# Seven half-size products in the output projection of a hybrid decoder step

## The chip, the core and the metric

The kernel runs on one core of a Trainium2 chip: TensorE (PE, with PEld for the weight loads that overlap it), VectorE (DVE), ScalarE (ACT), GpSimd (POOL), and SyncE (SP), which issues all DMAs of this kernel in one queue. The metric is device time in microseconds, median of several executions. Before the change it is 2507.13 us (three runs, 2505.12 to 2507.76).

## What is computed

One layer of a decoder with 16 heads of three kinds, over 1024 prompt tokens (with 16 meta tokens ahead of them) and 8 x 8 sample tokens, in float32. Every column comes from one input projection; after the heads comes the output projection, to which the change belongs, then the residual and a final norm.

```python
    h = _rmsnorm(x, norm_w)
    proj = jnp.einsum('bld,de->ble', h, w_in)
    (aq, ak, av, ao, ai, af, bq, bk, bv, ba, bb, cq, cf, ci, z) = jnp.split(proj, SPLIT_POINTS, axis=-1)
...
    hcat = jnp.concatenate([ha, hb, hc], axis=2)
    hcat = hcat * lax.rsqrt(jnp.mean(hcat * hcat, axis=-1, keepdims=True) + EPS)
    y = hcat.reshape(bsz, L, MIX) * out_norm_w.astype(f32) * jax.nn.silu(z.astype(f32))
    out = jnp.einsum('ble,ed->bld', y.astype(x.dtype), w_out)
    return x + out, (st_a[0], st_a[1], st_a[2], st_b, new_conv, st_c)
...
    y_prompt = _rmsnorm(xp[:, N_META:], final_norm_w)
    y_sample = _rmsnorm(xs, final_norm_w)
```

w_out is 2048 x 2048: 16 heads of 128 rows by four column groups of 512.

## The kernel before

**Precision.** Each float32 operand of a large product is split into a high and a low part in a format that TensorE takes at one pass, and a product is the sum of three matmuls: high·high, high·low and low·high. A weight block of 128 x 512 is loaded as a tile wraw (`o_raw` for w_out, `w_raw` for w_in), cast to whi on ACT and subtracted to wlo on DVE (`feed_split`). `pieces` lists all blocks in order of use; `feed_ahead` keeps three of them split and seven loaded or asked for ahead of the one in use, in four buffers each.

**Stages.** The prompt goes through in two halves of 512 tokens (`Half`; the first one also holds the sample and meta tokens). For each half `run_group` computes the input projection head by head, in the fixed ORDER (17 entries, "C3" the last), from the normalized transposed input hT/hB into PSUM tiles acc. While TensorE goes on with the next head, the last head's recurrence runs as a *stream*: a Python generator (`mlstm_scan`, `gdn_scan`, `hgrn_scan`, then `finish`) that gives out a few instructions at each step. `Weave` holds four queues of such streams (scan, fin, post, bg); `pump`, called between matmuls, takes a step when its due time on the estimated clock `ck` has come, and `drain` runs streams to their end. The build then fixes the order on each engine from the order of the source and from when its own model has an instruction ready, so a load can stand well ahead of its place in the source. bg holds `prep_B`, which prepares the second half's input in the first part of the run with tiles px and pxs.

**Finish.** `finish` scales one head's output by its norm, turns it around through DRAM (yd), multiplies by the gate into y, splits y into high (cast on ACT) and low (subtraction on POOL), and stores both parts to `y_dram`.

**Output projection.** `load_y` brings a half's y back, two heads to a tile, into the buffers h that held hT; the first half's comes in during the last input group, the second half's during the fourth unit. Then nine units (OUT_UNITS): for the first half four column groups with five token tiles each (one of samples), for the second half four with four tiles, of which the last is cut into two of two tiles. A unit runs over 16 heads; each weight block serves all its tiles:

```python
                    T.matmul(accs[n], yh, whi, start=k == 0, stop=False)
                    T.matmul(accs[n], yh, wlo, start=False, stop=both and k == NK - 1)
                    if not both:
                        T.matmul(accs[n], yl, whi, start=False, stop=k == NK - 1)
```

The samples' high and low parts share one stationary block, so they need two matmuls. A unit's accumulators (oacc, one PSUM bank of eight each) are added on DVE to a block of the input x (tile res), squared and summed on ACT, and multiplied by the final norm's weights on POOL. After a half's last column group `final_norm` scales the blocks and stores them.

## Time and profile before

| | us |
|---|---|
| median of 3 runs | 2507.13 |
| the profiled execution, its own time | 2506.0 |
| its span, first to last instruction | 2504.3 |
| mean granted TensorE clock | 0.990 |
| first half (input projection, heads) | 0 to about 1166 |
| second half | about 1166 to 2102.3 |
| output projection (first to last oacc matmul) | 2102.3 to 2493.9 |
| from the last matmul to the end | 10.4 |

All operations go through one helper, so all lines of the profile carry L137 and groups are told apart by the tile they write. A group's row reads: line, engine, operation, output <- inputs, shapes, count, then busy time, the mean of one in ns, and the idle time of the engine just before it with what ended it. A row of a window reads: start and end, length, then busy time and count for PE, PEld, DVE, ACT, POOL (of one tile's instructions alone where a tile is asked for), granted clock, DMA share and GB/s. Busy times of matmuls overlap each other, since they are pipelined.

### The profile page before, as it was taken

How to read it: one execution, taken by the hardware profiler on the slowest of the kernel's cores; microseconds unless marked ns; L12 is line 12 of the kernel's file. 1: busy time of each engine (PE TensorE's matmuls, PEld its weight loads, DVE VectorE, ACT ScalarE, POOL GpSimd, SP SyncE). 2: the span in 40 equal slices, each digit the busy share in tenths (PEclk: the TensorE clock that was granted, in tenths of full speed). 3: DMA queues.
4: the chain of work that ended last, by engine and by line, in shares of the span. 5: the costliest groups of instructions: out<-in, count | busy, mean ns of one | idle time of the engine just before them, and what ended most of it. 6: DMA issues, size and time to landing. Idle time of an engine off the chain costs nothing.

```text
span 2504.3 us, 43941 instructions
## 1 busy us (share of the span) xinstructions
PE 2442.1 (98%) x16032; PEld 2184.5 (87%) x16032; DVE 1425.5 (57%) x3080; ACT 991.2 (40%) x2430; POOL 554.8 (22%) x743
## 2 busy tenths in 40 slices
PE   6999999999999999999999999999999999999998
PEld 5898999999999999999787888888888888888886
DVE  7775655765656655556864556554654545323435
ACT  5643434443435333333642434333443334222324
POOL 5331212420313312113320113110320102211201
PEclk9999999999999999999999999999999999999999
DMA  5656665655645454447554455454554558636735
GB/s 129 152 140 147 147 146 133 162 131 130 158 99 138 99 131 118 118 119 203 132 132 115 120 123 136 122 130 101 138 127 114 129 123 257 183 84 200 254 97 185
DMA packets 681045, 350.82 MB, mean 140 GB/s; under 512 B 260004, under 2 KB 622076, under 8 KB 680828
## 3 DMA queue, kind: packets, MB, share of 16 engines
q1 hardware_dynamic: 680828, 348.01, 54.3%
q8 instruction: 126, 2.06, 0.4%
q14 instruction: 91, 0.75, 0.1%
HBM read 285.71 MB, written 62.19 MB: 139 GB/s over the span
## 4 chain that ended last, share of the span: by engine, by line
PE 80%; issue 5%; DVE 5%; DMA 4%; ACT 2%; POOL 2%; SPq 1%; POOLq 0%; DVEq 0%; ACTq 0%
PE acc L137 59%; PE oacc L137 9%; PE pa L137 1%; DVE wlo L137 1%; PE po L137 1%; PE nd L137 1%; PE pz L137 1%; PE pyy L137 1%; DMA wraw<-in_w_in_dram 1%; POOL res L137 1%; PE pu L137 1%; DMA px<-in_x_prompt_dram 1%; ACT whi L137 1%; PE poh L137 1%; PE pw L137 1%
## 5 line engine op out<-in xcount | busy, mean ns | idle before, releaser
L137 DVE TENSOR_TENSOR wlo<-wraw,whi 128x512 fp32r<-128x512 f32 x720 | 525.6, 734 | 569.6 <-ACT whi L137 552.1
L137 PE MATMUL acc<-hA,whi 128*128 128x288 f32 (+1 forms) x4544 | 826.2, 304 | 11.3 <-ACT whi L137 6.4
L137 ACT CAST whi<-wraw 128x512 fp32r<-128x512 f32 x720 | 441.9, 618 | 929.1 <-PE acc L137 641.2
L137 PE MATMUL acc<-hB,whi 128*128 128x512 f32 x2272 | 722.2, 400 | 4.3 <-ACT whi L137 2.1
L137 PEld LDWEIGHTS acc<-hA,whi 128*128 128x128 f32 x4544 | 679.6, 191 | 18.2 <-ACT whi L137 8.1
L137 PE MATMUL acc<-hA,wlo 128*128 128x288 f32 x2240 | 489.7, 299 | 1.6 <-DVE wlo L137 1.6
L137 PEld LDWEIGHTS acc<-hB,whi 128*128 128x128 f32 x2272 | 413.6, 189 | 86.2 <-ACT whi L137 2.7
L137 PE MATMUL acc<-hB,wlo 128*128 128x512 f32 x1120 | 441.1, 394 | 2.6 <-DVE wlo L137 2.6
L137 PEld LDWEIGHTS acc<-hA,wlo 128*128 128x128 f32 x2240 | 367.7, 190 | 2.7 <-DVE wlo L137 2.6
L137 PE MATMUL oacc<-whi,y 128*128 128x512 f32 x1088 | 343.4, 390 | 1.1 <-ACT whi L137 1.1
L137 PEld LDWEIGHTS acc<-hB,wlo 128*128 128x128 f32 x1120 | 211.0, 188 | 52.0 <-DVE wlo L137 6.8
L137 PEld LDWEIGHTS oacc<-whi,y 128*128 128x128 f32 x1088 | 204.2, 188 | 44.5 <-ACT whi L137 2.4
L137 PE MATMUL oacc<-wlo,y 128*128 128x512 f32 x576 | 224.8, 390 | 1.2 <-DVE wlo L137 1.2
L137 PEld LDWEIGHTS oacc<-wlo,y 128*128 128x128 f32 x576 | 108.1, 188 | 25.2 <-DVE wlo L137 3.1
L137 POOL TENSOR_TENSOR res<-res,fnw 128x512 f32<-128x512 f32 (+1 forms) x34 | 54.3, 1627 | 255.4 <-ACT oscr L137 255.4
L137 POOL TENSOR_TENSOR y<-y,zs 128x592 fp32r<-128x592 f32 (+1 forms) x32 | 46.0, 1437 | 171.4 <-ACT zs L137 106.7
L137 POOL TENSOR_TENSOR qd<-qT,emb 128x512 f32<-128x512 f32 x12 | 17.7, 1479 | 230.3 <-PE po L137 230.3
L137 DVE TENSOR_TENSOR Yt<-Yc,Bb 128x60 f32<-128x60 f32 (+8 forms) x180 | 37.6, 209 | 43.9 <-DMA Bb<-db 39.0
L137 POOL TENSOR_TENSOR hr<-hr,halfneg 128x4 f32<-128x4 f32 (+1 forms) x48 | 44.1, 919 | 61.1 <-DVE hr L137 58.4
L137 POOL TENSOR_TENSOR nrm<-nrm,halfneg 128x10 f32<-128x10 f32 x12 | 23.5, 1960 | 138.9 <-DVE nrm L137 138.9
L137 POOL TENSOR_TENSOR X<-Ex,hk 128x256 f32<-128x256 f32 (+1 forms) x40 | 39.1, 978 | 63.2 <-PE pa L137 41.8
L137 ACT ACTIVATE Wt<-pw,nrm 128x128 f32<-128x128 f32 (+1 forms) x54 | 19.8, 367 | 78.1 <-PE pw L137 78.1
(416 smaller groups left out, 2766.7 us busy)
## 6 DMA issues: line engine op xcount, KB each, us to landing
wraw<-in_w_in_dram SPq DMA_DIRECT2D x564, 256.0 KB
wraw<-in_w_out_dram SPq DMA_DIRECT2D x144, 256.0 KB
y<-y SPq DMA_DIRECT2D x16, 576.0 KB
px<-in_x_prompt_dram SPq DMA_DIRECT2D x32, 256.0 KB
yd<-y SPq DMA_DIRECT2D x128, 64.0 KB
out_dram<-sst SPq DMA_DIRECT2D x16, 512.0 KB
s<-yd SPq DMA_DIRECT2D x32, 256.0 KB
y<-zs SPq DMA_DIRECT2D x32, 256.0 KB
```

The lines of the kernel that those rows point to most:

```text
L137: return f(out, *a, **k)
```

## The change

The output projection of the 1024 prompt tokens is written as a product of 2 x 2 blocks: rows A1x, A2x are the two token halves, columns of A and rows of B the two sets of heads K1 (the first eight in ORDER) and K2 (the other eight), columns of B two pairs of column groups. Seven products of half size and sums give the four result blocks:

- S1 = A21 + A22, S2 = S1 - A11, S3 = A11 - A21, S4 = A12 - S2, in `finish` of the second half, from unsplit copies of y kept in `y_whole`; S1 to S4 and A22 are then split and stored in `y_comb`. The split's subtraction is now on DVE for these.
- T1 = B12 - B11, T2 = B22 - T1, T3 = B22 - B12, T4 = T2 - B21 (up to the order of subtraction in the code), on POOL, in a new bg stream `combine_weights` during the second half, stored in `w_comb`.
- The products, in order: A11·B11, A12·B21, S2·T2, S1·T1, S4·B22, S3·T3, A22·T4. Each is two units (j = 0, 1) of four tiles over eight heads; the last unit is cut in two. The sample tokens' rows are not combined: their matmuls ride along with the first three products, sharing a weight block (`own`) or with one of their own (`other`), so there they use one or two banks more.
- `load_y` brings in the next left factor while another one is in use. Partial results t1 and q stay in SBUF, and the input x is added at different places, by DVE or POOL.

```diff
-OUT_UNITS = ([(cg, range(5)) for cg in range(4)], [(cg, range(4)) for cg in range(3)] + [(3, range(2)), (3, range(2, 4))])
+HEADS = [{"A": 0, "B": HA, "C": HA + HB}[name[0]] + int(name[1]) for name in ORDER[1:]]
+K1, K2 = HEADS[:NH // 2], HEADS[NH // 2:]
+LAST_UNITS = [(0, range(4)), (1, range(2)), (1, range(2, 4))]
...
+    def c_raw(name, j, kk):
+        raw = wp.tile([P, 512], F32, tag="wraw", name="wraw")
+        DMA(raw, w_comb[name][NK // 2 * j + kk])
+        return raw
...
+    w_comb = {n: dp.tile([NK, P, 512], F32, name=n) for n in ("T1", "T2", "T3", "T4")}
+    y_comb = {n: dp.tile([NK // 2, P, 2 * HALF], F32R, name=n) for n in ("S1", "S2", "S3", "S4", "A22")}
+    y_whole = [dp.tile([n, P, HALF], F32, name=f"yw{n}") for n in (NH, NK // 2)]
...
-    for units in OUT_UNITS:
-        for cg, _ in units:
-            for k in range(NK):
-                pieces.append((o_raw, k, cg))
+    def out_pieces(j, rows, cg):
+        return [(o_raw, head, cg) for head in rows]
+    for j in range(2):
+        pieces += out_pieces(j, K1, j)
+    for j in range(2):
+        for a, b in zip(out_pieces(j, K2, j), out_pieces(j, K1, j + 2)):
+            pieces += [a, b]
+    for j in range(2):
+        for kk, b in enumerate(out_pieces(j, K2, j + 2)):
+            pieces += [(c_raw, "T2", j, kk), b]
+    for j in range(2):
+        pieces += [(c_raw, "T1", j, kk) for kk in range(NK // 2)]
+    for j in range(2):
+        pieces += out_pieces(j, K2, j + 2)
+    for j in range(2):
+        pieces += [(c_raw, "T3", j, kk) for kk in range(NK // 2)]
+    for j, _ in LAST_UNITS:
+        pieces += [(c_raw, "T4", j, kk) for kk in range(NK // 2)]
...
+        if not half.first:
+            kk, upper = HEADS.index(head) % (NK // 2), head in K1
+            ya = sp.tile([P, 512], F32, tag="vx0", name="ya", bufs=1)
+            if not upper:
+                yb = sp.tile([P, 512], F32, tag="vx1", name="yb", bufs=1)
+                yc = sp.tile([P, 2, 512], F32, tag="sst", name="yc", bufs=1)
+                yc, spare = yc[:, 0], yc[:, 1].bitcast(F32R)
...
+        if not half.first:
+            DMA(ya, y_whole[0][K1[kk]])
+            if not upper:
+                DMA(yb, y_whole[1][kk])
+                DMA(yc, y_whole[0][head])
...
+        if half.first:
+            DMA(y_whole[0][head], y[:, 0:HALF])
+            S.copy(yhi[:, 0:W], y[:, 0:W])
+            yield
+            yield
+            G.tensor_tensor(ylo[:, 0:W], y[:, 0:W], yhi[:, 0:W], op=ALU.subtract)
+            yield
+            d = y_dram[head].bitcast(F32)
+            for part, t in enumerate((yhi, ylo)):
+                t = t.bitcast(F32)
+                DMA(d[:, 2 * NSAMP + HALF * part:2 * NSAMP + HALF * (part + 1)], t[:, 0:HALF])
                 DMA(d[:, NSAMP * part:NSAMP * (part + 1)], t[:, HALF:WS])
+            return
+        y, yhi = y[:, 0:HALF], yhi[:, 0:HALF]
+        def parts(src, hi, name):
+            S.copy(hi, src)
+            ck.sync()
+            V.tensor_tensor(src.bitcast(F32R), src, hi, op=ALU.subtract)
+            d = y_comb[name][kk].bitcast(F32)
+            ck.last += 1.0
+            yield
+            DMA(d[:, 0:HALF], hi.bitcast(F32))
+            DMA(d[:, HALF:], src)
+        if upper:
+            DMA(y_whole[1][kk], y)
+            G.tensor_tensor(ya, ya, y, op=ALU.subtract)
+            yield
+            yield from parts(ya, yhi, "S3")
+            return
+        G.tensor_tensor(yb, yb, y, op=ALU.add)
+        yield
+        yield from parts(y, yhi, "A22")
+        G.tensor_tensor(ya, yb, ya, op=ALU.subtract)
+        yield
+        yield from parts(yb, spare, "S1")
+        G.tensor_tensor(yc, yc, ya, op=ALU.subtract)
+        yield
+        yield from parts(ya, yhi, "S2")
+        yield
+        yield from parts(yc, spare, "S4")
...
+    def load_y(u, n, src):
+        t = hp.tile([P, 2, 2 * NSAMP + 2 * HALF], F32R, tag=f"h{2 * u + n // 2}{n % 2}", name=f"y{u}{n}")
+        for q in range(2):
+            kk = 2 * n + q
+            if isinstance(src, str):
+                DMA(t[:, q, 2 * NSAMP:].bitcast(F32), y_comb[src][kk].bitcast(F32))
+            else:
+                DMA(t[:, q].bitcast(F32), y_dram[src[kk]].bitcast(F32))
+        yT[u][n] = t
+    def y_block(u, kk, n, part):
+        at_ = 2 * NSAMP + HALF * part + P * n
+        return yT[u][kk // 2][:, kk % 2, at_:at_ + P]
+    def combine_weights():
+        for j in range(2):
+            for kk in range(NK // 2):
+                b11, b12, b21 = (sp.tile([P, 512], F32, tag="px", name="px", bufs=3) for _ in range(3))
+                b22 = sp.tile([P, 512], F32, tag="pxs", name="pxs", bufs=1)
+                for t, heads, cg in ((b11, K1, j), (b12, K1, j + 2), (b22, K2, j + 2), (b21, K2, j)):
+                    DMA(t, i["w_out"][0, P * heads[kk]:P * (heads[kk] + 1), 512 * cg:512 * (cg + 1)])
+                for dst, a, b in ((b11, b12, b11), (b12, b22, b12), (b22, b22, b11), (b21, b21, b22)):
+                    ck.last = ck.t["T"] + 7.0
+                    yield
+                    G.tensor_tensor(dst, a, b, op=ALU.subtract)
+                ck.last = ck.t["T"] + 4.0
+                yield
+                for n, t in (("T1", b11), ("T3", b12), ("T2", b22), ("T4", b21)):
+                    DMA(w_comb[n][NK // 2 * j + kk], t)
+                ck.last = ck.t["T"] + 10.0
+                yield
...
+            weave.add("bg", combine_weights())
...
+    def phase(u, accs, tiles, own=None, other=None, each=None):
+        for kk in range(NK // 2):
+            whi, wlo = next_piece()
+            for n in tiles:
+                yh, yl = (y_block(u, kk, n, part) for part in (0, 1))
+                T.matmul(accs[n], yh, whi, start=kk == 0, stop=False)
+                T.matmul(accs[n], yh, wlo, start=False, stop=False)
+                T.matmul(accs[n], yl, whi, start=False, stop=kk == NK // 2 - 1)
+                if n == tiles[0]:
+                    feed_ahead()
+                weave.pump()
+            for job in (own, other):
+                if not job:
+                    continue
+                if job is other:
+                    whi, wlo = next_piece()
+                a, block = job
+                T.matmul(a, block(kk), whi, start=kk == 0, stop=False)
+                T.matmul(a, block(kk), wlo, start=False, stop=kk == NK // 2 - 1)
+                if job is other:
+                    feed_ahead()
+                weave.pump()
+            if each:
+                each(kk)
+    def banks(tiles=halfn):
+        return {n: bank("oacc") for n in tiles}
...
+    t1, q = {}, {}
+    for j in range(2):
+        accs, sacc = banks(), bank("oacc")
+        phase(0, accs, halfn, own=(sacc, lambda kk: yT[0][kk // 2][:, kk % 2, 0:2 * NSAMP]))
+        ck.begin()
+        if j == 0:
+            weave.drain_queue("bg")
+            for n in halfn:
+                t1[j, n] = sp.tile([P, 512], F32, tag="px" if n < 3 else "pxs", name="t1", bufs=3 if n < 3 else 1)
+                S.copy(t1[j, n], accs[n])
+            held = sacc
+    weave.drain_queue("scan")
+    weave.drain_queue("fin")
+    weave.drain_queue("post")
+    ys = [row(tag, "ys", F32R)[:, 0:512] for tag in "aabb"]
...
+    fnw += [sp.tile([P, 512], F32, tag=f"s{t}", name="fnw", bufs=1) for t in ("7", "8", "9", "B")]
+    ck.begin()
+    for n in halfn:
+        t1[1, n] = free.pop(0)
+        S.copy(t1[1, n], accs[n])
+    for t, c in zip(fnw, range(4)):
+        DMA(t, i["final_norm_w"][512 * c:512 * (c + 1)].rearrange("(x d) -> x d", x=1).partition_broadcast(P))
+    for c in range(4):
+        DMA(ys[c].bitcast(F32).rearrange("p (h c) -> p h c", h=4), y_dram[4 * c:4 * (c + 1), :, 0:2 * NSAMP].bitcast(F32).rearrange("h p c -> p h c"))
+    def ys_block(heads):
+        return lambda kk: ys[heads[kk] // 4][:, P * (heads[kk] % 4):P * (heads[kk] % 4 + 1)]
+    sample_add(0, held, False)
+    sample_add(1, sacc, False)
+    weave.add("bg", norm_states())
+    for j in range(2):
+        accs, sacc, sacc2 = banks(), bank("oacc"), bank("oacc")
+        def each(kk):
+            if j == 0 and kk in (1, 3, 5):
+                load_y(0, kk // 2, "S2")
+        phase(1, accs, halfn, own=(sacc, lambda kk: yT[1][kk // 2][:, kk % 2, 0:2 * NSAMP]), other=(sacc2, ys_block(K1)), each=each)
+        weave.drain_queue("bg")
+        for n in halfn:
+            t = res[n + 1, j] = x_load(n + 1, j)
+            ck.begin()
+            V.tensor_tensor(t, t, accs[n], op=ALU.add)
+            G.tensor_tensor(t, t, t1[j, n], op=ALU.add)
+            squared(n + 1, j)
+        sample_add(j, sacc, True)
+        sample_add(j + 2, sacc2, False)
+    for j in range(2):
+        accs, sacc = banks(), bank("oacc")
+        def each(kk):
+            if j == 0 and kk == 1:
+                load_y(0, 3, "S2")
+            if j == 0 and kk in (3, 5, 7) or j == 1 and kk == 1:
+                load_y(1, kk // 2 - 1 if j == 0 else 3, "S1")
+        phase(0, accs, halfn, other=(sacc, ys_block(K2)), each=each)
+        for n in halfn:
+            ck.begin()
+            V.tensor_tensor(t1[j, n], t1[j, n], accs[n], op=ALU.add)
+        sample_add(j + 2, sacc, True)
+    free += [row(tag, "res")[:, 0:512] for tag in "aabb"]
+    weave.add("post", final_norm([0], range(4)))
+    for j in range(2):
+        accs = banks()
+        def each(kk):
+            if j == 0 and kk % 2:
+                load_y(0, kk // 2, "S4")
+        phase(1, accs, halfn, each=each)
+        for n in halfn:
+            q[j, n] = free.pop(0)
+            ck.begin()
+            V.tensor_tensor(q[j, n], t1[j, n], accs[n], op=ALU.add)
+    weave.drain_queue("post")
+    for j in range(2):
+        accs = banks()
+        def each(kk):
+            if j == 0 and kk % 2:
+                load_y(1, kk // 2, "S3")
+        phase(0, accs, halfn, each=each)
+        for n in halfn:
+            t = res[n + 1, j + 2] = free.pop(0)
+            ck.begin()
+            V.tensor_tensor(t, q[j, n], accs[n], op=ALU.add)
+            x = x_load(n + 1, j + 2)
+            G.tensor_tensor(t, t, x, op=ALU.add)
+            free.append(x)
+            squared(n + 1, j + 2)
+            x = x_load(n + 5, j)
+            G.tensor_tensor(t1[j, n], t1[j, n], x, op=ALU.add)
+            free.append(x)
+    weave.add("post", final_norm(range(1, 5), range(4)))
+    for j in range(2):
+        accs = banks()
+        def each(kk):
+            if j == 0 and kk % 2:
+                load_y(0, kk // 2, "A22")
+        phase(1, accs, halfn, each=each)
+        for n in halfn:
+            t = res[n + 5, j + 2] = q[j, n]
+            ck.begin()
+            V.tensor_tensor(t1[j, n], t1[j, n], accs[n], op=ALU.add)
+            V.tensor_tensor(t, t, accs[n], op=ALU.add)
+            x = x_load(n + 5, j + 2)
+            G.tensor_tensor(t, t, x, op=ALU.add)
+            free.append(x)
+            squared(n + 5, j + 2)
+    weave.drain_queue("post")
+    for j, tiles in LAST_UNITS:
+        accs = banks(tiles)
+        phase(0, accs, tiles)
+        weave.drain_queue("post")
+        late = tiles[-1] == NC - 1 and j == 1
+        for n in tiles:
+            t = res[n + 5, j] = t1[j, n]
+            ck.begin()
+            V.tensor_tensor(t, t, accs[n], op=ALU.add)
+            squared(n + 5, j, late)
+        if j == 1:
+            weave.add("post", final_norm([n + 5 for n in tiles], (2, 3, 0, 1), late))
     weave.drain_queue("bg")
     weave.drain_queue("post")
```

140 lines of the change are left out of this document (52 added, 88 removed).

## Prediction

> **What bounds the kernel now.** I read the page first (busy shares, the chain that ended last), then the groups of instructions, then TensorE's waits, then windows of the stage that the change rewrites.
>
> ```profile
> span 2504.3 us, 43941 instructions
> PE 2442.1 (98%) x16032; PEld 2184.5 (87%) x16032; DVE 1425.5 (57%) x3080; ACT 991.2 (40%) x2430; POOL 554.8 (22%) x743
> PE 80%; issue 5%; DVE 5%; DMA 4%; ACT 2%; POOL 2%; SPq 1%; POOLq 0%; DVEq 0%; ACTq 0%
> L137 PE MATMUL oacc<-whi,y 128*128 128x512 f32 x1088 | 343.4, 390 | 1.1 <-ACT whi L137 1.1
> L137 PE MATMUL oacc<-wlo,y 128*128 128x512 f32 x576 | 224.8, 390 | 1.2 <-DVE wlo L137 1.2
> ```
>
> TensorE is busy 98% of the span and holds 80% of the last chain; no other engine passes 57%. The output projection is the tile oacc: 1088 + 576 = 1664 matmuls of 128x512, with 1.1 + 1.2 us of idle time in front of them. The mean of 390 ns is the length of one in the pipeline, not the pitch, so the pitch comes from windows. The waits of TensorE from 2100 us to the end, the oacc row with its first and last start, and then four windows of the tile oacc (length, busy time and count of PE, PEld, DVE and ACT, clock, DMA share, GB/s):
>
> ```profile
> PE oacc L137 <- DVE wlo L137: 1.2, 5, 0.3
> PE oacc L137 <- ACT whi L137: 1.1, 3, 0.7
> ```
> ```profile
> L137 PE MATMUL oacc<-whi,y x1088: 387/389/529, 2102.3 to 2493.5; 128*128 128x512 f32 x182
> ```
> ```profile
> 2203.10:2253.50 50.40, 50.40 (x224) 41.72 (x223) 3.22 (x5) 0.58 (x1) 1.00 0.32 84
> 2253.50:2303.90 50.40, 50.40 (x224) 41.75 (x223) 3.22 (x5) 0.58 (x1) 1.00 0.60 187
> 2310.00:2330.20 20.20, 19.82 (x87) 15.84 (x85) 3.22 (x5) 0.58 (x1) 1.00 0.59 185
> 2472.00:2493.90 21.90, 20.28 (x83) 14.89 (x81) 0.67 (x1) 0.00 (x0) 1.00 0.65 207
> ```
>
> 224 matmuls take 50.40 us: 225 ns each, with nothing between them, although each of the first two windows holds a change of unit. So in this stage a matmul less is 225 ns less, as long as the weight pieces, the evacuations and the transfers keep up. Only the end is worse: 83 matmuls in 21.90 us, where the pitch asks 18.7.
>
> **The change: what goes.** Before, 8 prompt tiles x 16 heads x 4 column groups x 3 products (hi·hi, hi·lo, lo·hi) = 1536 matmuls, plus 128 for the samples. After, 7 products x 2 column groups x 4 tiles x 8 heads x 3 = 1344, plus the same 128. That is 1472, and 192 fewer: 192 x 0.225 = **43.2 us**. The pieces go from 144 to 152; each needs a cast on ACT and a subtraction on DVE as before, and I cost them at nothing, since TensorE spends at least 1.35 us on a piece of 6 matmuls and 3.2 us on a pair of pieces of 14.
>
> **What is added beside the second token half** (1215 to 2102 us). The window over all engines, the groups that do the same operations today, the DMA issue of a weight block, and a window of the first half, which already carries a background stream through px:
>
> ```profile
> 1215.00:2102.00 887.00, 881.53 (x4936) 728.16 (x4936) 501.42 (x1047) 340.99 (x803) 158.87 (x180) 1.00 0.52 131
> L137 POOL TENSOR_TENSOR y<-y,zs 128x512 fp32r<-128x512 f32 (+1 forms) x16 | 21.4, 1338 | 123.8 <-ACT zs L137 76.9 <-DMA wraw<-in_w_in_dram 45.4 <-issue 1.5
> L137 DVE TENSOR_TENSOR wlo<-wraw,whi 128x512 fp32r<-128x512 f32 x274 | 202.4, 743 | 194.1 <-ACT whi L137 188.0 <-PE acc L137 3.6 <-DMA hvT<-hvT 1.4
> L137 ACT CAST zs<-y x32: 604/646/689, 203.3 to 2171.9; 128x592 fp32r<-128x592 f32 x16, 128x512 fp32r<-128x512 f32 x16
> wraw<-in_w_out_dram SPq DMA_DIRECT2D x144, 256.0 KB
> 400.00:676.00 276.00, 273.37 (x2194) 269.00 (x2193) 177.52 (x404) 114.91 (x309) 78.29 (x107) 0.98 0.62 146
> ```
>
> - The weight combinations: 16 rounds of 4 POOL subtractions, 64 x 1.34 = 86 us. The heads: 8 upper ones keep one POOL operation, 8 lower ones have three for one, 16 x 1.34 = 21 us. POOL goes from 159 to 266 of 887 us, 30%.
> - The splits: 8 + 8 x 4 = 40 on DVE (30 us, 501 to 531) and 24 casts more on ACT (16 us).
> - DMA: 16 x 8 blocks of 0.262 MB = 33.6 MB for the weights; the heads load and store 31.5 MB where they stored 8.4. Together 57 MB more, 131 to 195 GB/s, and some 220 issues more in SP's queue. (In the first half 16 blocks are stored more, 4.2 MB in 1100 us; I count nothing.)
>
> None of it is in TensorE's stream; what hides it is the 881.5 us of matmuls and a fetch of seven pieces ahead. If the cover fails, the longer chains of a head (up to four splits one after the other at its end, which hold the zs and y buffers longer) reach the next head's scan, and SP's queue, standing at a store that waits for POOL, holds back the weight loads behind it. The lower bound is nothing. For the upper one I take the window 400 to 676, at 28% POOL and 146 GB/s: 2.63 us idle and a clock of 0.98, thus 8.2 us lost in 276, where this half loses 5.5 in 887. Carried over, 26 us less 5.5, about 20. I take 3, near the low end, since this half has 40% of DVE's time free.
>
> **What is added in the output stage.** There are 15 units where there were nine, and sums that stay in SBUF: 56 DVE additions from PSUM for 32, and 62 POOL operations on prompt tiles for 30. Today's durations, by tile and by group from 2100 us:
>
> ```profile
> L137 DVE TENSOR_TENSOR res<-res,oacc x36: 671/679/689, 2160.4 to 2493.9; 128x512 f32<-128x512 f32 x32, 64x512 f32<-64x512 f32 x4
> L137 POOL TENSOR_TENSOR res<-res,fnw 128x512 f32<-128x512 f32 x30 | 46.4, 1568 | 255.4 <-ACT oscr L137 255.4
> ```
>
> DVE: four evacuations of 0.68 us in a unit of 21.6 us. POOL is thickest in the fifth product: 24 x 1.57 = 38 of 43 us. It lags there without holding a bank, because DVE's addition frees the bank and x is added afterwards. The narrow places are the second product, whose unit takes six of the eight banks (before, five), and the end of the first, where four copies on ACT free the banks behind the last head's finish. The next unit can start in the two free banks; two tiles are 1.35 us of matmuls, and the old unit's first tile ends 2.9 us ahead of the unit's end, so a bank comes free in time unless its addition waits for an x block. A change of unit costs 0 in the two clean windows and 0.6 us (20.20 less 87 x 0.225) where the old stage passed from one half to the other. For 14 changes that is 0 to 8 us; I take 3, the rows lying nearer to nothing.
>
> The tail: the last two units have 8 pieces instead of 16, so seven of eight are fetched before the unit starts. That can win back the 3.2 us lost today; or the outputs of the two tiles before (2.1 MB, 6.4 us at 328 GB/s) stand ahead of the last outputs and cost up to 6. I take +1. The chain from the last matmul (2493.9) to the end, 10.4 us, stays.
>
> **The sum.** The profiled execution took 2506.0 us, 1.7 more than its span and 1.1 below the median of the three (2507.13). 2506.0 - 43.2 + 3 + 3 + 1 = 2469.8, so **2470 us**.
>
> **Transfers, the price that could undo it.** Per product, in MB (pieces + y blocks + x and outputs) and us of matmuls: second 13.9 to 18 (with ys, the norm weights and the last head's blocks) in 57.7; third 13.6 in 50.4; fourth 8.9 in 43.2; fifth 12.6 in 43.2; sixth 14.7 in 43.2; seventh 8.4 in 43.2. That is 312, 270, 206, 292, 340 and 194 GB/s at most, where the old stage has 168 on average. The busiest windows today and the whole stage, all engines; then a window with a clock below 1 and TensorE's waits in it; then a piece of the chain that ended last (start, length):
>
> ```profile
> 2330.20:2363.00 32.80, 32.79 (x145) 27.15 (x146) 14.53 (x25) 10.76 (x23) 2.39 (x2) 1.00 0.94 328
> 2340.00:2350.00 10.00, 10.00 (x46) 8.29 (x45) 2.77 (x4) 2.84 (x5) 0.00 (x0) 1.00 0.98 361
> 2102.00:2504.00 402.00, 389.54 (x1768) 320.75 (x1767) 162.79 (x263) 131.91 (x260) 78.05 (x62) 0.99 0.55 168
> 580.00:680.00 100.00, 98.14 (x808) 96.07 (x809) 60.02 (x146) 37.68 (x105) 22.58 (x37) 0.95 0.58 139
> ```
> ```profile
> PE pz L137 <- DVE Yc L137: 2.2, 1, 2.2
> ```
> ```profile
> 2478.12 5.50 DMA wraw<-in_w_out_dram
> ```
>
> 328 GB/s for 32.8 us with TensorE never idle: the load exists today and costs nothing. The Trainium skill (DMA: Bandwidth & Descriptors, Specifications) puts the limit of HBM for one core at about 358 GB/s; the 361 of the 10 us window agrees with it as a ceiling. By that figure no product is bound by transfers, and the sum would stay.
>
> **The rivals.**
> 1. *Transfers bind in the output stage; slower.* If only a rate R is reached, a product lasts MB/R: at 0.25 the second, third, fifth and sixth lose 14.3 + 4.0 + 7.2 + 15.6 = 41 us, so at about 248 GB/s the gain is gone. At the 207 of the tail, in which the last chain runs through 5.50 us of a weight load, they lose 29.3 + 15.3 + 17.7 + 27.8 = 90: 2506.0 - 43.2 + 90 = 2553; halfway, at 228, about 2527. For it: y blocks of half a megabyte stand ahead of weight pieces in one queue, and idle time lowers the clock (0.95 in the window with the 2.2 us wait). Against it: the 328 above, and most y blocks have a whole unit of slack. Chance 0.12.
> 2. *The second half's side work reaches TensorE.* The upper price of 20 us in place of 3: 2487. For it, the longest chain of a head grows by some 15 us of splits; against it, 18% to 30% of POOL and free DVE. Chance 0.20.
> 3. *Nothing new waits, and the tail's 3.2 us come back:* 2506.0 - 43.2 - 3.2 = 2459.6. Chance 0.08.
>
> That the products are not fewer is excluded by the count.
>
> The Trainium skill (SBUF — State Buffer, Who interferes with whom) speaks against the change: a DVE operation with two SBUF inputs and a POOL operation that reads SBUF lock each other out. By it, the added 80 POOL operations could hold up DVE by as much as 107 us in the second half, an estimate from the 1.34 us above. It is a reason for rival 2; the rows do not show how much of it happens, only that the split's mean is 743 ns.
>
> **How the numbers follow.** Forecast 0.60, rivals 0.12, 0.20, 0.08. The range: 2458 (just under rival 3) to 2495 (rival 2 with 8 us of bank waits on top) leaves out rival 1 and the worst of rival 2. A difference of 0.2%, 5 us, is about what a measurement of this kernel can tell. Faster: forecast, rival 3, 0.17 of rival 2, together 0.85. Same 0.05: 0.03 of rival 2 and 0.02 of rival 1 near 248 GB/s. Slower: the other 0.10.
>
> **What would show it.** oacc with 1472 matmuls at 225 ns and under 3 us more of idle time; the stage from the first oacc to the last near (2493.9 - 2102.3) - 43.2 + 4 = 352 us, and its first matmul near 2105 (2102 today). Rival 1 shows as TensorE or ACT waiting for DMA into wraw in the second or sixth product at 0.9 DMA share; rival 2 as oacc starting after 2115. Wrong altogether would be a matmul count above 1472, or idle time ahead of oacc that names PSUM evacuations at every unit.

## The result and the profile after

After the change the kernel takes 2597.34 us (median of 4, 2593.72 to 2599.89) against 2506.12 (median of 4, 2504.26 to 2507.76): 1.0363 times the time before, interval 1.0345 to 1.0381. It is **slower**, by 91 us, where 2470 was forecast. The page of the kernel after, with the busy shares, the chain that ended last and the oacc groups:

```profile
span 2591.8 us, 44367 instructions
PE 2431.7 (94%) x15840; PEld 2166.3 (84%) x15840; DVE 1520.3 (59%) x3160; ACT 1011.7 (39%) x2474; POOL 706.5 (27%) x855
PE 8%; DMA 2%; POOL 2%; issue 1%; DVE 1%; ACT 1%; SPq 0%; POOLq 0%; DVEq 0%; ACTq 0%
L137 PE MATMUL oacc<-whi,y 128*128 128x512 f32 x928 | 300.7, 398 | 16.0 <-ACT whi L137 15.9
L137 PE MATMUL oacc<-wlo,y 128*128 128x512 f32 x480 | 191.7, 399 | 11.2 <-DVE wlo L137 11.2
```

TensorE has its 192 matmuls fewer (15840 for 16032; oacc 928 + 480 and 64 for the samples) and is busy 10 us less, yet the span is 87.5 us longer: it now stands still, 97.9 us more than before. What runs on it runs slower, too: the count alone would take 43.2 us off the busy time, so by this estimate the matmuls that are left took some 33 us longer (mean granted clock 0.973, before 0.990). Ahead of oacc the idle time is 27.2 us where it was 2.3. (Here the chain could be followed back only through a small part of the span, so the shares of its row are of no use.) Cut into stages, from the first matmul on hB and the first and last on oacc:

| us | first half | second half | output stage | span |
|---|---|---|---|---|
| before | 1165.7 | 936.6 | 391.2 | 2504.3 |
| after | 1225.8 | 969.0 | 386.1 | 2591.8 |
| difference | +60.1 | +32.4 | -5.1 | +87.5 |

So the largest loss lies in a stage for which the prediction counted nothing. The k-th matmul on acc, compared between the two traces, is level (+1.5 us) up to 714 us of the kernel before; the gap is +60.1 us at 1000 us and +63.6 at 1580. What runs there in the kernel after, by the tile px (operation, count, shortest/median/longest in ns, first and last start):

```profile
L1755 SPq DMA_DIRECT2D px<-in_w_out_dram x48: 327/418/711, 698.5 to 991.2; - x48
L137 POOL TENSOR_TENSOR px<-px x16: 1262/1298/2002, 703.3 to 994.8; 128x512 f32<-128x512 f32 x16
```

These are the weight sums. The source adds `combine_weights` when the second half begins (1226 us in this run), but they need only w_out and the buffers px, which are free at 698 us, and the build put all of them there. The same 304 us before and after, all engines:

```profile
697.00:1001.00 304.00, 302.96 (x2544) 296.92 (x2544) 182.74 (x440) 119.39 (x326) 77.79 (x107) 1.00 0.48 118
```
```profile
697.00:1001.00 304.00, 258.40 (x2085) 249.50 (x2085) 165.29 (x356) 95.84 (x258) 148.33 (x151) 0.93 0.72 206
```

POOL goes from 77.79 to 148.33 us, TensorE from 2544 matmuls to 2085, at a clock of 0.93. Who waited there in the kernel after: TensorE, SP's queue and POOL (total, times, longest):

```profile
PE puh L137 <- ACT t L137: 13.6, 1, 13.6
PE acc L137 <- DVE wlo L137: 7.9, 3, 4.6
PE pz L137 <- DVE X L137: 7.7, 1, 7.7
PE pz L137 <- DVE s L137: 6.1, 1, 6.1
```
```profile
SPq L1763 <- POOL px L137: 45.2, 28, 4.1
```
```profile
POOL px L137 <- DMA px<-in_w_out_dram: 50.3, 10, 9.2
POOL px L137 <- DMA pxs<-in_w_out_dram: 30.8, 9, 9.0
```

Two in-order queues stand still: POOL 81 us in front of loads of the weight sums, SP 45 us in front of their stores (L1763). What TensorE names are links of the heads' recurrences (puh, pz) and a late split. Two of its waits, followed back in the timeline (start, length, and in brackets the idle time of the engine before):

```profile
735.70 1.29 POOL L137 TENSOR_TENSOR px<-px 128x512 f32<-128x512 f32 x1 [5.34 <-DMA px<-in_w_out_dram]
741.86 0.56 POOL L137 TENSOR_TENSOR hr<-hr,halfneg 80x1 f32<-80x1 f32 x1
742.45 0.29 DVE L137 TENSOR_TENSOR t<-t,hr 80x128 f32<-80x128 f32 x1 [10.19 <-POOL hr L137]
743.37 1.08 PE L137 MATMUL pz<-s,Ball 64*64 64x64 f32 x8 [6.13 <-DVE s L137]
```
```profile
890.92 1.26 POOL L137 TENSOR_TENSOR px<-px 128x512 f32<-128x512 f32 x1 [5.93 <-issue]
892.12 0.20 POOL L137 COPY un<-U 128x24 f32<-128x24 f32 x1
892.36 0.70 ACT L137 ACTIVATE U<-Cq 128x592 f32<-128x592 f32 x1 [17.45 <-POOL un L137]
893.78 0.79 PE L137 MATMUL puh<-meta,t 80*128 80x128 f32 x2 [13.57 <-ACT t L137]
```

In both, a small operation of a head (hr, un) stands in POOL's queue behind subtractions of the weight sums that wait for their loads. DVE or ACT stands at it, with TensorE's operand behind it in that engine's own queue. From 690 to 1010 us DVE waits 33.2 us for POOL's hr, where it waited 8.8 before, and ACT 26.1 us for un, where it did not wait at all. The wait of 4.6 us for wlo follows an hr in the same way. The one of 7.7 us is that of a head's solver, whose inputs nm and Bb came late from DRAM (DVE stood 9.24 and 3.25 us for them).

### The profile page after: what moved, and what is told of

Same layout as the page of the kernel before. It is cut to its first block, busy times and chain, and to the rows that moved or that the text cites. A ratio compares the mean times of both kernels' runs of the same rounds, so it can differ in the third digit from the quotient of the medians.

```text
span 2591.8 us, 44367 instructions
## 1 busy us (share of the span) xinstructions
PE 2431.7 (94%) x15840; PEld 2166.3 (84%) x15840; DVE 1520.3 (59%) x3160; ACT 1011.7 (39%) x2474; POOL 706.5 (27%) x855
## 5 line engine op out<-in xcount | busy, mean ns | idle before, releaser
L137 PE MATMUL acc<-hA,whi 128*128 128x288 f32 (+1 forms) x4544 | 830.6, 305 | 17.5 <-ACT whi L137 10.0
L137 DVE TENSOR_TENSOR wlo<-wraw,whi 128x512 fp32r<-128x512 f32 x728 | 553.3, 768 | 469.2 <-ACT whi L137 437.6
L137 PE MATMUL oacc<-whi,y 128*128 128x512 f32 x928 | 300.7, 398 | 16.0 <-ACT whi L137 15.9
L137 PEld LDWEIGHTS oacc<-whi,y 128*128 128x128 f32 x928 | 177.7, 192 | 56.0 <-ACT whi L137 18.8
L137 PE MATMUL oacc<-wlo,y 128*128 128x512 f32 x480 | 191.7, 399 | 11.2 <-DVE wlo L137 11.2
L137 PEld LDWEIGHTS oacc<-wlo,y 128*128 128x128 f32 x480 | 92.3, 192 | 35.7 <-DVE wlo L137 16.6
L137 POOL TENSOR_TENSOR res<-res,fnw 128x512 f32<-128x512 f32 (+1 forms) x30 | 42.2, 1417 | 60.7 <-ACT res L137 59.8
L137 POOL TENSOR_TENSOR res<-res 128x512 f32<-128x512 f32 x24 | 34.9, 1464 | 86.6 <-DVE res L137 66.4
L137 POOL TENSOR_TENSOR X<-Ex,hk 128x256 f32<-128x256 f32 (+1 forms) x40 | 38.9, 973 | 58.1 <-PE pa L137 35.8
L137 PE MATMUL pz<-X,Ball 32*32 32x32 f32 x576 | 19.7, 204 | 36.8 <-DVE X L137 28.0
```

The lines of the kernel that those rows point to most:

```text
L137: return f(out, *a, **k)
```

## The experiments

The theory after the comparison: the products save what was counted, and the sums cost more, through the engines and in-order queues that they share with the heads' recurrences and the weight feed. The rivals: the transfers (57 MB more) do it, or merely the place of the weight sums. Each time below is that of one execution with a profile; the kernel before took 2497.87 to 2506.58 us beside them, so a few microseconds between two kernels tell nothing. All stages, in us:

| run | first half | second half | output | time |
|---|---|---|---|---|
| e1_no_weight_sums | 1167.7 | 969.9 | 387.8 | 2537.99 |
| e3_no_token_sums | 1218.6 | 940.2 | 364.3 | 2535.78 |
| e5_no_sums | 1159.5 | 934.3 | 367.5 | 2473.86 |
| e4_no_sums_dve_adds | 1158.8 | 933.0 | 348.4 | 2452.67 |
| e2_weight_sums_late | 1164.8 | 1013.5 | 384.4 | 2575.45 |
| f1_weight_sums_pool_queue | 1261.2 | 974.5 | 385.4 | 2634.27 |
| f3_weight_moves_only | 1184.0 | 967.2 | 384.5 | 2548.84 |
| f4_weight_pool_only | 1216.7 | 978.3 | 388.0 | 2595.80 |
| f9_weight_memset_only | 1178.8 | 970.8 | 388.3 | 2550.79 |
| f7_weight_sums_dve | 1200.1 | 983.2 | 383.2 | 2579.13 |
| f6_token_sums_pool_queue | 1164.1 | 970.5 | 379.7 | 2527.04 |
| r1_token_loads_late | 1167.0 | 967.2 | 387.3 | 2534.24 |
| r3_token_moves_only | 1169.1 | 951.8 | 372.8 | 2506.39 |
| r4_token_arith_only | 1161.9 | 974.3 | 370.5 | 2519.56 |
| r2_weight_sums_dve_paced | 1159.3 | 967.1 | 347.6 | 2486.60 |
| g2_all_sums_dve | 1202.5 | 970.9 | 366.6 | 2553.08 |
| g3_dve_paced_complete | 1168.6 | 987.4 | 366.5 | 2535.23 |
| g4_token_stores_pool_queue | 1170.4 | 994.5 | 360.8 | 2538.38 |

### Taking the parts out

e1 drops the stream and reads blocks of w_out in place of T1 to T4; e3 drops the token sums, and the products read A22 in place of S1, S2 and S4; e5 drops both.

```diff
-            weave.add("bg", combine_weights())
...
-        pieces += [(c_raw, "T1", j, kk) for kk in range(NK // 2)]
+        pieces += out_pieces(j, K1, j)
```
```diff
-                load_y(0, kk // 2, "S2")
+                load_y(0, kk // 2, "A22")
```

> The weight sums are left out: T1 to T4 are plain blocks of w_out. Theory (the build hoisted the sums into 698 to 1001 us of the first half, where POOL and SP stand in order behind their transfers): the second half's first matmul comes back from 1225.8 to about 1166, the rest stays, total about 2597 - 60 = 2537 (2530 to 2545). Rival (the loss is elsewhere and the sums only happen to run there): the second half still starts after 1200, total above 2570.

> The sums of y are left out: every head of the second half is split once as in the kernel before, and S1, S2, S4 are the A22 blocks, S3 the A21 block. Theory (the heads' longer ends hold up the next heads and SP's queue): second half from 969 us back to about 937, output stage 10 to 20 us shorter than its 386, first half still 1226: total 2545 to 2555. Rival (the second half's 32 us come from elsewhere, such as the order that the build chose): second half stays above 960, total above 2580.

> Both kinds of sums left out; the seven products and the new output stage remain. Theory: first half 1166, second 937, output stage 365 to 375 because its head-end stores are gone but ACT still waits for POOL's additions: total 2485 to 2495. Rival A (the new output stage is slow by itself): the stage stays near 386, total about 2505. Rival B (only the sums hurt it): the stage takes about 352 as predicted, total about 2468.

The weight sums cost 58.1 us in the first half (1225.8 - 1167.7) and nothing elsewhere. The token sums cost 8.2 + 35.6 + 20.3 us (e1 less e5). With neither, the kernel takes 2474 us. That this is close to the forecast is in part luck: 19.1 us that additions on POOL cost in the output stage (e4, below) meet 8.5 us that the two halves gain and that nothing explains. e3 and e5 came out 9 and 11 us below the totals expected of them. The seven products were not the trouble, then; the sums were.

### The weight sums: place, transfers, POOL

e2 ties each round to the second half: a copy of one column from the last split into each px buffer before its load. f3 keeps only the loads and stores; f4 only the subtractions, on px buffers filled once; f9 is f4 with memsets in place of the subtractions, which write but read nothing.

```diff
+                for t in (b11, b12, b22, b21):
+                    G.tensor_copy(t[:, 0:1], splits[at[0] - 1][0].bitcast(F32)[:, 0:1])
```
```diff
-                    G.tensor_tensor(dst, a, b, op=ALU.subtract)
+                    G.memset(dst, 0.0)
+                    G.memset(dst, 0.0)
+                    G.memset(dst[:, 0:256], 0.0)
```

> The same sums and bytes, but each round's four loads are tied by a one-column POOL copy from the weight block then in use, so that they can't run before the second half. Theory (place and queue order, not bytes): second half starts at about 1166, and the sums cost at most 20 us there: total 2537 to 2557. Rival (bytes: 76 MB more in all, whoever carries them): total stays within 10 us of 2597.

> The 64 loads and 64 stores of the weight sums stay on SP, the 64 POOL subtractions are left out (each block is stored as loaded). Theory P: without POOL in it the first half falls to about 1175, total about 2545. Theory S in its wider form (any store in SP's queue that waits for something slow): SP now waits for each load to land, the first half stays above 1200. Theory of bytes: above 1215.

> The 64 subtractions stay on POOL, on tiles that are set once; the 128 transfers are left out and T1 to T4 are plain blocks of w_out. Theories P and S both say that POOL's 83 us of arithmetic cost little by themselves: first half 1166 to 1178, total 2538 to 2550. Rival (POOL's arithmetic is what the heads wait for): first half above 1200, total above 2570.

> Like f4 (no transfers, plain blocks for T1 to T4), but each POOL subtraction is replaced by memsets of about the same length in all, which read nothing from SBUF. Theory L (POOL's reads and DVE's two-input operations lock each other out, so that the solver's 0.2 us operations take 1.3 us): POOL as busy as in f4, but the first half falls from 1216.7 to about 1170 and the total to about 2540. Theory Q (the heads' own POOL operations wait behind the added ones in POOL's queue): nothing changes against f4, first half above 1205, total about 2590.

e2: the first half is level again, but the second loses 43.6 us more than e1's, where 20 were expected at most. Part of it can be the tie's: its 64 copies run on POOL too, which stood 60.6 us in front of them for the cast of a weight block. Even so, nothing shows the sums to be cheap where the prediction had put them. f3: the transfers alone cost 16.3 us. f4: POOL's arithmetic alone costs 49.0 us, with no transfer at all, against both theories. Without transfers the 64 subtractions run back to back from 697 to 791 us; the first of the four kinds, by the tile px in f4:

```profile
L137 POOL TENSOR_TENSOR px<-px x16: 1256/1283/1744, 696.8 to 786.4; 128x512 f32<-128x512 f32 x16
```

The window 690 to 800 of e1, f4 and f9, all engines, and in each the group of DVE in which the solver of a head's recurrence multiplies and subtracts (Yc):

```profile
690.00:800.00 110.00, 110.00 (x944) 107.56 (x944) 61.66 (x167) 47.34 (x127) 19.91 (x28) 1.00 0.46 113
```
```profile
L137 DVE TENSOR_TENSOR Yc<-Yc,Yt 128x75 f32<-128x75 f32 (+14 forms) x15 | 3.0, 201 | 0.4
```
```profile
690.00:800.00 110.00, 68.94 (x555) 66.12 (x553) 67.89 (x92) 19.84 (x55) 94.43 (x78) 0.77 0.23 54
```
```profile
L137 DVE TENSOR_TENSOR Yc<-Yc,Yt 128x75 f32<-128x75 f32 (+14 forms) x15 | 16.2, 1080 | 0.4
```
```profile
690.00:800.00 110.00, 101.75 (x849) 99.00 (x848) 55.68 (x153) 36.89 (x105) 74.04 (x168) 0.94 0.42 103
```
```profile
L137 DVE TENSOR_TENSOR Yc<-Yc,Yt 128x75 f32<-128x75 f32 (+14 forms) x15 | 3.0, 200 | 0.4
```

The same 15 small operations take 201 ns each in e1, 1080 beside POOL's subtractions, and 200 beside memsets. In f4 each of them ends up nearly as long as one of POOL's (1.28 us), as if the two engines took turns. TensorE, which needs the solver's result and the splits, gets through 555 matmuls instead of 944. Its waits in f4, same window:

```profile
PE pz L137 <- DVE s L137: 16.8, 1, 16.8
PE acc L137 <- DVE wlo L137: 11.9, 1, 11.9
PE pz L137 <- DVE X L137: 11.8, 1, 11.8
```

With memsets 11.1 of the 49.0 us stay, though POOL works as long for them: between 640 and 800 us it is busy 75.7 us more than in e1, in f4 75.3. (They begin at 655 us, some 40 us sooner, and are shorter pieces.) So most of f4's loss goes when POOL's added work reads nothing: it comes with a lock between POOL's reads and DVE's operations with two inputs. Not all of it is the lock: the wait of 16.8 us lies behind a head's hr in POOL's queue, at which DVE stood 18.93 us (12.41 in f9). The Trainium skill (SBUF — State Buffer, Who interferes with whom) states this lock, and that it does not hold for a POOL instruction that only writes; both halves agree with the Yc rows above.

In the kernel after, the subtractions are spread over 300 us by their loads, and the lock weighs less. From 697 to 1001 us the solver's operations are as short as in e1, where their mean is 216 ns:

```profile
L137 DVE TENSOR_TENSOR Yc<-Yc,Yt 128x75 f32<-128x75 f32 (+14 forms) x30 | 6.5, 215 | 0.9
```

The longest group, wlo, has a mean of 814 ns there for 712 before, some 6 us over its 62 operations; all of DVE's operations together take some 19 us more than at their means in e1, spread over the 304. What TensorE's longest waits lead to is the place of the heads' operations in POOL's queue, as followed back above. Two more kernels test it: f1 issues the sums' transfers from POOL instead of SP, f7 does the subtractions on DVE.

```diff
-                    DMA(w_comb[n][NK // 2 * j + kk], t)
+                    nc.gpsimd.dma_start(w_comb[n][NK // 2 * j + kk], t)
```
```diff
-                    G.tensor_tensor(dst, a, b, op=ALU.subtract)
+                    V.tensor_tensor(dst, a, b, op=ALU.subtract)
```

> The weight sums unchanged, but their 128 transfers are issued from POOL's queue instead of SP's. Theory S (SP stands at stores that wait for POOL, and the loads of the heads and weights wait behind): the first half falls from 1226 to about 1180, total about 2552. Theory P (POOL stands at its blocks' loads, 81 us, and the heads' POOL operations wait behind it): the first half stays above 1215, since POOL waits for the same loads, total about 2590.

> The complete change, with the 64 subtractions of the weight sums on DVE instead of POOL. Theory L: no lock, so the first half is about that of the moves alone (1184) plus a few us for 44 us of DVE work: 1185 to 1195, total 2550 to 2560. Rival (DVE standing at the loads holds up wlo): first half above 1215, total above 2580.

f1 is the worst of all, 35.4 us behind the kernel after in the first half and 44 above the total that its second theory gave. That theory's mechanism holds: SP no longer stands at the stores, but POOL, which the recurrences need, now issues and waits as well, and DVE waits 45.6 us for hr. f7 wins 25.7 us in the first half, 5 to 15 short of what its theory gave, and gives 14.2 back in the second. With the sums off POOL, DVE waits 6.5 us for hr and ACT no longer for un; instead DVE's own queue stands 26.6 us at the sums' loads. So of the 58 us some 26 go when the sums leave POOL (its queue, and what the lock had), some 16 stay with the transfers alone (f3), and the other 16 are what f7 loses against f3 by subtracting on DVE. f4's 49.0 us are no part of this sum, since its subtractions run in a row.

### The output stage: additions in front of ACT

e4 is e5 with the four places of `t + x`, `t + t1` and `t1 + x` on DVE.

```diff
-            G.tensor_tensor(t, t, x, op=ALU.add)
+            V.tensor_tensor(t, t, x, op=ALU.add)
```

> Both kinds of sums left out as in e5 (output stage 367.5, total 2473.9), and the additions of x and t1 in the output stage on DVE instead of POOL. Theory (ACT's squares wait for POOL's additions, and the weight casts stand behind them in ACT's queue): output stage about 355, total about 2461. Rival (the 19 us above the ideal 348 come from banks and transfers): stage stays above 364, total above 2470.

The output stage of e5 and of e4, all engines, then TensorE's waits in each from the stage's start to its end, and ACT's in e5:

```profile
2093.00:2462.00 369.00, 355.19 (x1579) 289.80 (x1577) 202.87 (x294) 140.10 (x276) 116.50 (x92) 0.98 0.69 219
```
```profile
PE oacc L137 <- DVE wlo L137: 10.3, 7, 3.7
PE oacc L137 <- ACT whi L137: 3.1, 3, 1.2
```
```profile
ACT res L137 <- POOL res L137: 41.1, 20, 4.2
```
```profile
2092.00:2441.00 349.00, 346.21 (x1574) 284.07 (x1572) 216.49 (x324) 140.03 (x275) 78.15 (x60) 1.00 0.73 231
```
```profile
PE oacc L137 <- DVE wlo L137: 1.5, 3, 0.9
PE oacc L137 <- ACT whi L137: 0.8, 1, 0.8
```

348.4 us is the stage before less the matmuls that go: 391.2 - 43.2 = 348.0. The additions on POOL cost 19.1 us. None of TensorE's waits names an evacuation, so they hold no bank, as the prediction said. But the square that follows on ACT waits for them (41.1 us, 20 times), and the casts of the next weight pieces stand behind the square in ACT's queue; for res on POOL or DVE, ACT waits 55.3 us in all in e5 and 30.7 in e4. A second effect goes with it: the splits wlo, for which TensorE waits most, have a mean of 849 ns in e5, 772 in e4 and 754 before, 12 us in all between e5 and e4. That fits the lock of f4; no run parts the two. The row of e4 also settles the transfers: the products' y blocks, weights, x and outputs all pass in this stage, at 231 GB/s on average, and TensorE is busy for 346.21 of 349 us.

### The token sums

f6 issues their transfers from POOL; r1 keeps them on SP but ties the loads to the moment when the head's scaled output is in y (a copy of one column, as in e2); r3 keeps the transfers and leaves the sums and extra splits out; r4 keeps sums and splits and leaves the transfers out. All four are without the weight sums and stand beside e1.

```diff
+            for t in (ya,) if upper else (ya, yb, yc):
+                V.tensor_copy(t[:, 0:1], y[:, 0:1])
```
```diff
-        G.tensor_tensor(yb, yb, y, op=ALU.add)
+        hr = hrs[-1].rearrange("p c t -> p (c t)")
+        G.tensor_tensor(yb, hr, y, op=ALU.add)
```

> No weight sums (left out as in e1), and the transfers of the token sums (in both halves) are issued from POOL's queue. Compared with e1 (second half 969.9, output stage 387.8, total 2538). Theory S: SP no longer stands at the heads' stores and loads: second half about 940, output stage about 370, total about 2485 to 2495. Rival (the longer chains themselves, on ACT, DVE and POOL, hold up the next head): second half above 960, total above 2525.

> No weight sums (as e1: second half 969.9, output stage 387.8, total 2538); the token sums complete, but the loads of ya, yb and yc are tied by a one-column DVE copy to the moment when the head's output has been turned, so that they can't stand in SP's queue right behind the previous head's stores. Theory H (SP stands at a hoisted yc load whose buffer is still being stored, and the next head's gate rows and solver blocks wait behind it): second half 950 or less, total about 2515. Rival C (the longer chain on ACT, DVE and POOL itself): second half stays above 962.

> Left out: the weight sums, and of the token sums the arithmetic and the extra splits: each head of the second half is split once, and that one pair is stored to the places of A22, S1, S2 and S4 (upper heads: S3); all loads and stores of the token sums stay, so the prompt's output is not the reference's. Compared with e1_no_weight_sums (second half 969.9, output stage 387.8, total 2538) and e5_no_sums (934.3, 367.5, 2473.9). Theory C, the longer chain of a head holds the next one back: second half at most 945, output stage at most 375. Rival, the transfers and SP's queue do it: second half at least 960, output stage at least 380.

> Left out: the weight sums, and of the token sums the transfers: loads of ya, yb, yc, the stores of whole y and those of S1, S2 and S4; the sums and splits stay on their engines but take the head's own turned output in place of what was loaded, and the products read A22 in place of S1, S2 and S4, so the prompt's output is not the reference's. Compared with e1_no_weight_sums (second half 969.9, output stage 387.8) and e5_no_sums (934.3, 367.5). Theory C, the longer chain of a head: second half at least 960. Rival, the transfers: second half at most 945, since POOL's and DVE's instructions alone cost little. Output stage, by theory C: 380 or more; by the rival, at most 375.

In the second half the longer work at a head's end is the cause: r4, with no transfers, loses 40.0 us against e5, more than e1 does (35.6), while another queue (f6, 970.5) or later loads (r1, 967.2) change little. The transfers alone cost 17.5, between the two expectations of r3, so the two do not add up. Whether the chain's length, POOL's queue or the lock counts most was not parted; POOL has a share, since moving the token sums to DVE as well shortens this half by 12.3 us from f7 to g2 (below). Where it shows is the start of a head's solver. The largest stall of the second half in the kernel after, from the timeline, then TensorE's waits in the second half in r4 and in e5:

```profile
1981.10 1.35 PE L137 MATMUL pz<-X,Ball 32*32 32x32 f32 x32 [14.13 <-DVE X L137]
```
```profile
PE pz L137 <- DVE X L137: 13.8, 4, 9.6
PE acc L137 <- DVE wlo L137: 9.4, 6, 4.0
```
```profile
PE acc L137 <- DVE wlo L137: 2.7, 4, 1.1
PE acc L137 <- ACT whi L137: 2.1, 2, 1.9
PE pz L137 <- DVE X L137: 2.1, 2, 1.7
```

In the output stage neither part does it alone (r3 372.8, r4 370.5, for 367.5 without and 387.8 with both), so r4's expected 380 or more is a miss. What has both is a store that waits for a late split. SP's queue around the start of the stage in the kernel after, and TensorE's longest wait there followed back:

```profile
SPq L932 <- ACT zs L137: 20.1, 2, 10.7
```
```profile
2225.98 0.42 ACT L137 ACTIVATE Ex<-Sx 128x256 f32<-128x256 f32 x1 [10.94 <-POOL X L137]
2226.76 0.60 ACT L137 CAST zs<-ya 128x512 fp32r<-128x512 f32 x1
2227.39 0.32 SPq L932 DMA_DIRECT2D S<-zs  x1
2231.76 1.93 SPq L245 DMA_DIRECT2D wraw<-in_w_out_dram  x4
2235.99 0.62 ACT L137 CAST whi<-wraw 128x512 fp32r<-128x512 f32 x1 [7.07 <-DMA wraw<-in_w_out_dram]
2236.66 0.80 PE L137 MATMUL oacc<-whi,y 128*128 128x512 f32 x1 [6.84 <-ACT whi L137]
```

ACT stands 10.94 us for the last head's X, the cast of a token sum (zs) comes behind that in its queue, SP stands at the store of this cast (L932), and the first weight blocks of the stage come behind the store. In e1 the row of L932 reads 19.2 us and TensorE's longest wait is 6.8 as well; in r3 and r4 L932 has 8.6 and 5.7 us, and no wait of TensorE on oacc passes 3.7. This explains that wait, not all of the 20 us: g4, below, puts these stores on POOL's queue and changes the stage by no more than one execution can tell (5.7 us).

### Versions with all sums

r2 is e4 with the weight sums back, on DVE and tied to the second half as in e2. g2 is the whole change with every sum and addition on DVE; g3 adds the ties of e2 and r1; g4 adds to g3 the token sums' stores on POOL's queue.

> Only the weight sums remain (the token sums left out as in e3, output additions on DVE as in e4, which took 2452.7): on DVE, paced over the second half by DVE copies from the weight block in use. Theory (most of the sums' price is the lock with POOL and the bunching): second half 933 + 10 to 20, output stage 348 to 352, total 2463 to 2475. Rival (moving 34 MB through SP's one queue costs by itself): total above 2485.

> The complete change with every sum (weights, tokens, output stage) on DVE. Theory L for all three places: first half about 1190, second half about 950, output stage about 368, total about 2520, still slower than before. If DVE's added work binds instead: total stays above 2560. Beating the kernel before (2506) would need the token sums' 35 us to be lock time as well.

> The complete change, all sums on DVE, weight sums paced over the second half, token loads tied. If both theories hold: first half 1160, second half 965, output stage 360 to 367, total 2497 to 2505, about level with the kernel before. If the pieces do not add up (DVE over 65% busy in the second half): above 2530.

> g3 with the stores of the split token sums issued from POOL's queue, so that SP does not stand at the last heads' stores while weight loads wait behind (in the output stage SP stood 24.6 us at them). Theory: output stage from about 365 to 352, total 10 to 15 us below g3. Rival: POOL's own work waits at those stores and the second half grows by as much.

r2: the weight sums still cost 34.1 us in the second half (967.1 for e4's 933.0), with no operation added on POOL and no token sums beside them. The total is 11.6 us above what the theory allowed and 1.6 above the rival's bound. DVE stands 24.1 us at the sums' loads there and SP 24.0 us at their stores; how much of the 34.1 these make was not tested. g2 wins 44 us on the kernel after, g3 62: 2535.23, and the kernel before beside it took 2502.89. Both are some 30 us above what was expected. g4 wins 5.7 us of the output stage and loses 7.1 in the second half, as its rival said. No complete version that was run beats the kernel before.

## Why the prediction was wrong

The whole difference of the spans divides along a ladder of kernels, each step one part: before 2504.3, e4 2451.0 (seven products alone: -53.3), e5 2472.2 (additions on POOL: +21.2), e1 2536.3 (token sums: +64.1), after 2591.8 (weight sums: +55.5). Of the -53.3, 42.8 lie in the output stage; the other 10.5 are in the halves, which should not differ; they are not explained and about as large as the spread of the kernel before.

- **What goes** was right: 1472 matmuls at 225 ns, 43.2 us forecast and 42.8 measured between before and e4 in the output stage.
- **"None of it is in TensorE's stream; what hides it is the 881.5 us of matmuls and a fetch of seven pieces ahead … I take 3"** is the step that failed, twice over. The place: the side work was set "beside the second token half" (1215 to 2102 us), but the weight sums ran at 698 to 1001, because nothing in their operands tied them there. The text ahead of the prediction says that the build can bring a load well forward, and the prediction did not apply this to the stream. The price: 3, at most 20, against 58 in the first half and 35.6 in the second. The cover counted weight pieces only, but TensorE also takes operands from the heads' recurrences (puh, pz), and these pass over POOL. The upper price was read from a window with POOL busy at 28%. A mean share says nothing of a head's operation that stands in POOL's queue behind subtractions and their loads: DVE and ACT stood 10.19 and 17.45 us at two such operations, each under 0.6 us long. And moving the sums to the expected place (e2) or off POOL as well (r2) still left 44 and 34 us, so the place alone was not the error. The prediction's own sign for this, oacc starting after 2115, came: it started at 2194.8.
- **Rival 2** had the right mechanism, and its sentence on the longer chain of a head and on SP's queue at a store names what r4 and the waits show. Its size was wrong: it was capped at 20 us. It looked at the second half alone, and at stores of SP rather than POOL's queue. The lock between DVE and POOL, the reason given for it, is real (f4) but did not touch the solver in the kernel after. With bounds of 0 and 107 us the honest course was still to leave that range open, not to cap it.
- **"It lags there without holding a bank"** was true and beside the point. The additions cost 19.1 us (e5 less e4) for the 3 taken, through ACT's queue and longer splits, not through a bank. The changes of unit themselves cost next to nothing: e4's waits ahead of oacc are 2.3 us in all.
- **Rival 1**, transfers, fell: 231 GB/s over the whole stage in e4 with TensorE busy throughout.
- **The first half's 16 stores** of whole y, counted at nothing, belong to the parts that cost 7.2 and 8.2 us there (after less e3, e1 less e5), hardly more than the spread.
- **The tail** stays as forecast: from the start of the last matmul to the end 10.9 us, before 10.8.

Open: what part of the 20 us that the token sums cost in the output stage goes with the store at L932, and how the weight sums come to cost 34 us on DVE.

## What to carry to other kernels

Side work is priced at the place where the build runs it, not where the source adds it: look for what its operands leave free, and tie it down if its place matters. An engine that is 20 to 30% busy is no cover where the critical recurrence runs over that engine's queue or shares its reads; price what can stand in front of one link, the operations and the loads that they wait for, not the mean share. And before an operation moves to a free engine, look at which in-order queue has to wait for it (here ACT's squares ahead of the weight casts, SP's stores ahead of the weight loads).

## What was not expected of the hardware

The size of the lock: in f4 DVE operations of 0.2 us took 1.08 us on average in a row of POOL subtractions of 1.28 us, and 0.2 beside memsets. And a pause costs twice. In r4 TensorE's waits in the second half add up to 30.8 us, in e5 to 9.0; the half is 40.0 us longer, at a granted clock of 0.97 for 1.00 (1230 to 2090 us). In the kernel after, the shortest, median and longest matmul on oacc:

```profile
L137 PE MATMUL oacc<-whi,y x928: 387/389/795, 2194.8 to 2580.9; 128*128 128x512 f32 x186
```

The longest is 2.04 times the median; before the change the longest of this group was 529. In f4 the granted clock fell to 0.77 over the 110 us that hold three waits of 11.8 to 16.8 us. The Trainium skill (TensorE: Matmul & The Clock Gate, What's actually happening) says that the clock falls to half after an idle window of about 3.4 us; the factor of 2.04 agrees, and the length of the window no run here shows.
